# Attention stage of a hybrid layer: the order of VectorE, ScalarE and SyncE written out by hand

## The chip, the cores and the metric

The kernel runs on one core of a Trainium2 chip, as one program. The metric is the device time of one execution in microseconds. A core has TensorE (PE: matmuls and transpositions; PEld: its weight loads), VectorE (DVE), ScalarE (ACT), GpSimd (POOL) and SyncE (SP), which issues most of the transfers. Every engine takes its own instructions in the order in which the program lists them, and waits at each one for its inputs and for its output buffer.

## The reference, cut to what matters

```python
mod = c @ w_ada + b_ada; shift, scale, gate = split(mod, 3)
h = rmsnorm(x, norm_g) * (1 + scale) + shift            # 1024 tokens x 1024
glu_a, glu_b, z_conv, q, k, v, z_att, g_conv, g_att = split(h @ w_in)
u = conv31(glu_a * sigmoid(glu_b)) + conv_b
y_conv = (silu(layernorm(u)) * silu(z_conv)) @ w_conv_out
q, k = rope16(q), rope16(k)                             # 24 heads of 64, first 16 columns rotated
for g, (window, dilation) in enumerate(((128, 1), (512, 4), (2048, 16))):   # 8 heads each
    o[g], m[g], den[g] = banded_softmax_attention(q, k, v, window, dilation)  # max and sum kept
wt[g] = den[g] * exp(m[g] - max(m));  att = sum(wt[g] * o[g]) / sum(wt[g])
y_att = (att * silu(z_att)) @ w_att_out
merged = sigmoid(g_conv) * y_conv + sigmoid(g_att) * y_att
out = rmsnorm(x + gate * (merged @ w_o), final_g)
```

## The kernel before, in words

All matmuls are done to nearly full float32 precision: each operand is split into a high part (a ScalarE `Copy` into the 32-bit matmul type) and a low part (original minus high, on VectorE, or on GpSimd for most projection weights), and three matmuls (high x high, high x low, low x high) are summed in one PSUM bank. `split` at L55 writes both parts; L57 is the Copy and L58 the subtraction. `mm3` (L73 to L75) is the three matmuls.

The program runs in stages: the modulation and the normed input (to about 100 us), the projections of the convolution branch with the convolution on VectorE, the first output projection (to 639 us), the attention stage (639 to 1148 us), a merge (to about 1192 us) and the last projection with its norm. The change lies in the attention stage and, with one instruction, in the merge.

The attention stage (L645 to L1060) is cut into slots. A slot on TensorE is half of a half of a projection unit: 4 of 8 blocks of the contraction, 12 matmuls of 512 columns. There are 32 units of 4 slots: 24 make k and q (two for each of the 12 pairs of heads; the pairs run over four columns of heads j and in each over the three dilation groups g), and the last 8 make the gate of the attention branch. `pieces` (L769) yields after each slot, and, where a half of a unit is complete, hands back a function `after` that takes the result out of its bank (two banks, `pd2`). For part 0 of k and q that is the rotary part on VectorE (L720 to L723: shuffle, two multiplies, an add) and then the split (L731, L732); part 1 is split only. In the next slot SyncE copies the parts into the stacked tiles that the scores read (`move_kq`, L796: five transfers for each head, L794), the second head's later.

From slot 0 on, a slot also carries one of 8 steps of the current pair (r = 0 to 7 below): the scores (L862, L863), with the minimum and mask on VectorE (L866) and two Exp on ScalarE (L870); two slots later (`turn`) a transposition of the probabilities into a bank `t` (L878) and their split (tiles `ph`, `pl`); four slots later (`values`) the product with v (L896 to L898), whose bank ScalarE copies out every second slot (L902). The banks `s`, `t` and `o` have two buffers each. `load_v` (L811) loads half of a pair's v and splits it for its two heads. `store_stats` writes row minima and sums to memory, and after each group 2 `combine` (L910) brings the three groups of a column together: it loads the statistics, computes weights (L918 to L928), transposes them (L932) into a `t` bank, stores them, loads them back as rows (tiles `wg`, tag `wr`, two buffers) and weighs the outputs (L953 to L964); the last column goes straight into the tiles of the next projection, the others through memory. `load_raw` loads weights into a ring of three buffers.

The loop that lays this out (L1017 to L1058) stands in `tc.manual_schedule(engines={nc.tensor.engine})`: TensorE's order is as written, and the order of the other engines is chosen by a planner with costs of its own. The beginning of the program has all of TensorE, VectorE, ScalarE and SyncE in written order.

In the merge (L1074 to L1088) each of 8 blocks of the attention projection is multiplied by its gate, which comes from memory, and added to the other branch.

Of the kernel before, what the change touches and what calls it, by code (L numbers as in the profile page):

```python
# [39 lines left out]
def layer(ctx: ExitStack, tc: tile.TileContext, a, out):  # L40
# [621 lines left out]
    for x, dt, n in (("sb", F32, 3), ("ph", F32R, 2), ("pl", F32R, 2)):  # L662
        ap_.tile([P, 512], dt, name=x, tag=x, bufs=n)
# [42 lines left out]
    made, parts_of = [], {}  # L706

    class Parts:
# [7 lines left out]
        def __call__(self, half, s, ps):  # L716
            src = ps
            if self.part == 0:
                sh, src = (ap_.tile([P, 512], F32, name=x, tag="gs", bufs=2) for x in ("sh", "rot"))
                nc.vector.stream_shuffle(sh, ps, SHUF)  # L720
                nc.vector.tensor_mul(src, ps, ctab[:, s])
                nc.vector.tensor_mul(sh, sh, stab[:, s])
                nc.vector.tensor_add(src, src, sh)  # L723
            r = (1, 4, 16)[self.g]
            n = 512 // r

            def dst(t):
# [3 lines left out]
            nc.scalar.activation(dst(self.hi), src, AF.Copy)  # L731
            nc.vector.tensor_sub(dst(self.lo), src, dst(self.hi).bitcast(F32))  # L732
            if half:
                parts_of[self.n, self.part] = self.parts
                made.append((self.n, self.part))

    def gate(d):
# [18 lines left out]
    def units():  # L756

        raws = kq_raws(0)
        gates = list(range(KT))
        for n in range(12):  # L760
            yield kq_weights(raws, 0), Parts(n, 0)
            w = kq_weights(raws, 1)
            if n + 1 < 12:
                raws = kq_raws(n + 1)
            yield w, Parts(n, 1)
        for d in gates:
            yield weights(a["w_t"][60 + d], lo_eng=nc.gpsimd), gate(d)

    def pieces():  # L769

        source = units()
        ahead = next(source)
        while ahead:
            (hi, lo), consume = ahead
            ahead = next(source, None)
            for half in range(2):
                s = slice(half * 512, half * 512 + 512)
                ps = bank()
                for k in range(KT):
                    c = slice(k * P, (k + 1) * P)  # L780
                    mm3(ps, hi[:, c], lo[:, c], hh[:, k, s], hl[:, k, s], k == 0, k == KT - 1)
                    if k == 3:
                        yield
                yield lambda half=half, s=s, ps=ps: consume(half, s, ps)
# [21 lines left out]
    def row_tile(name):  # L806
        return ap_.tile([P, 512], F32, name=name, tag="wr", bufs=2)
# [3 lines left out]
    def load_v(n, half):  # L811
# [14 lines left out]
        for h in range(2):  # L826
            if not half:
                v2[n, h] = stk.tile([P, 8, 2, 64], F32R, name="vt", tag=f"v{turn_of(n, h)}")
            hi, lo = (v2[n, h][:, 4 * half:4 * half + 4, x] for x in range(2))
            split(hi, lo, raw[:, :, 64 * h:64 * h + 64])  # L830
            yield

    class Attend:
# [19 lines left out]
        def scores(self, st_):  # L853
# [4 lines left out]
            sb = self.sb[st_] = ap_.tile([P, 512], F32, name="sb", tag="sb", bufs=3)  # L858
# [45 lines left out]
        def store_stats(self):  # L904
            by_token(sscr[self.j][:, self.g], self.stats.rearrange("p t h x -> p t (h x)"), self.g)
            yield
# [3 lines left out]
    def combine(j):  # L910
# [24 lines left out]
        nc.sync.dma_start(wscr[j].rearrange("g h (t p) -> (g h t) p", p=P), wt)  # L935
        yield

        def row_of(g, s):
            row = row_tile("wg")
            for h in range(2):  # L940
                nc.sync.dma_start(row[64 * h:64 * h + 64], wscr[j][g, h:h + 1, s].to_broadcast([64, 512]))
            return row

        o = [o_of.pop((j, g)) for g in range(3)]
        halves = [slice(0, 512), slice(512, 1024)]
        rows = row_of(0, halves[0]), row_of(1, halves[0])
        yield
        for half, s in enumerate(halves):
            o0 = o[0][:, s]
            o1 = o[1].rearrange("p (r b i) -> p b i r", r=4, b=2)[:, half]  # L950
            o2 = o[2].rearrange("p (t s i) -> p i t s", t=8, s=2)[:, 32 * half:32 * half + 32]
            w0, w1 = rows
            nc.vector.tensor_mul(o0, o0, w0)  # L953
            w2 = row_of(2, s)
            v = w1.rearrange("p (i r) -> p i r", r=4)
            nc.vector.tensor_mul(v, v, o1)
            nc.vector.tensor_add(o0, o0, w1)
            gt = row_tile("gt")
            nc.sync.dma_start(gt, zascr[j][:, s])
            yield  # L960
            v = w2.rearrange("p (i t s) -> p i t s", t=8, s=2)
            nc.vector.tensor_mul(v, v, o2)
            nc.vector.tensor_add(o0, o0, w2)
            nc.vector.tensor_mul(o0, o0, gt)  # L964
            if not half:
                rows = row_of(0, halves[1]), row_of(1, halves[1])
            if j < 3:
                nc.sync.dma_start(atscr[j][:, s], o0)
            else:
                att_parts(3, s, o0)  # L970
            yield
# [3 lines left out]
    def att_parts(j, s, raw):  # L975
# [3 lines left out]
        split(ah[j][:, s], al[j][:, s], raw)  # L979
# [4 lines left out]
    def w_out(n, kp, pool=None):  # L984

        raw = load_raw(a["w_o"][n, kp])
        if pool:
# [6 lines left out]
        split(hi, lo, raw)  # L994
        woh[n, kp], wol[n, kp] = hi, lo

    stream = pieces()


# [3 lines left out]
    STEPS = (2, 3, 4, 5, 7, 8, 9, 10, 11)  # L1003
    beside, heads = {}, {}
# [9 lines left out]
    def v_slots(n, half):  # L1014
        return [8 * n + x for x in ((2, 4, 5) if half else (-2, 0, 1))]

    with tc.manual_schedule(engines={nc.tensor.engine}):  # L1017
        for slot_ in range(-LEAD, (2 * len(order) + KT) * 4 - LEAD):
            due, made[:] = made[:], []
            after = next(stream)  # L1020
            for n, part in due:
                move_kq(n, part, 0)
                in_steps(moves(n, part, 1), [slot_ if n == 0 else slot_ + 1 if part else 8 * n - 4])
            for half in range(2):
                n = (slot_ + 2) // 8
                if slot_ == v_slots(n, half)[0] and 0 <= n < len(order):
                    in_steps(load_v(n, half), v_slots(n, half))
            if 0 <= slot_ < stages:
                n, st_ = divmod(slot_, 8)
                if st_ == 0:  # L1030
                    heads[n] = Attend(n)
                heads[n].scores(st_)
                if st_ == 7:
                    in_steps(heads[n].store_stats(), [slot_ + 1])
                    if order[n][1] == 2:
                        in_steps(combine(order[n][0]), [slot_ + 1 + x for x in STEPS])
# [5 lines left out]
            if TURN <= slot_ < stages + TURN:  # L1042
                n, st_ = divmod(slot_ - TURN, 8)
                heads[n].turn(st_)
            for c in beside.pop(slot_, ()):
                next(c)
            j = slot_ - stages - VAL
            if 0 <= j < 3:
                raw = load_raw(atscr[j])
                for half in range(2):  # L1050
                    s = slice(half * 512, half * 512 + 512)
                    att_parts(j, s, raw[:, s])
            if j in (4, 6, 8):
                w_out(0, j // 2 - 2)
            if j == 11:
                ahead = weights(a["w_ao"][0], 512)
            if after:
                after()  # L1058
        assert not beside and next(stream, None) is None
    c_ctx.close()  # L1060
# [14 lines left out]
    for d in range(KT):  # L1075
# [3 lines left out]
        if d in (1, 3, 5):  # L1079
            w_out(*((0, 3), (1, 0), (1, 1))[d // 2], fp if d > 1 else None)  # L1080
# [10 lines left out]
    w_out(1, 2, fp)  # L1091
    w_out(1, 3)
# [115 lines left out]
```

## Time and profile before

| what | value |
|---|---|
| runs shown: median (lowest to highest) | 1286.9 us (1286.76 to 1290.35) |
| the profiled execution, its own time | 1287.98 us |
| its span, first to last instruction | 1286.2 us |
| TensorE busy | 1243.6 us, 97% |
| VectorE busy | 915.3 us, 71% |
| ScalarE busy | 516.6 us, 40% |
| GpSimd busy | 94.7 us, 7% |
| mean granted clock of TensorE | 0.992 |
| the chain that ended last, by engine | PE 81%, DVE 7%, ACT 5%, DMA 4%, issue 2% |

A busy share is the time in which an engine has an instruction under way. Matmuls overlap, so TensorE's own durations are longer than the distance from one start to the next; starts are what to measure by. The wait list says for each line how long its engine stood before it and which engine or transfer released it. The releaser is the one that came last by the profile; where that one had long been done, it was another. The granted clock is the share of full speed that TensorE was given in a stretch.

### The profile page before, as it was taken

Reading aid. Unit: us, or ns where it says so; the run is one execution under the profiler, and the core shown is the slowest. Engines: PE = TensorE matmul, PEld = TensorE weight load, DVE = VectorE, ACT = ScalarE, POOL = GpSimd, SP = SyncE. Lnnn points to the kernel's source line nnn. Section 1 sums busy time; section 2 is a strip of 40 time slices with the busy share of each in tenths; the row PEclk is TensorE's granted clock in tenths of the full one; section 3 lists DMA queues with packets and bytes.
Section 4 is the critical chain, followed back from the end, with each engine's and each line's share of the span. In section 5 each row is a group of like instructions: output and inputs, shape, how many; then the busy total and the mean of one; then the engine's idle time right before and its main releaser. Section 6 shows DMA issues by size and latency. Waiting matters only on the chain.

```text
span 1286.2 us, 16854 instructions
## 1 busy us (share of the span) xinstructions
PE 1243.6 (97%) x6208; PEld 1041.9 (81%) x6208; DVE 915.3 (71%) x1496; ACT 516.6 (40%) x1027; POOL 94.7 (7%) x79
## 2 busy tenths in 40 slices
PE   6999999999999999999999999999989999899997
PEld 4787888888888888888788888878878878788886
DVE  6777999999999987843255657857866753339544
ACT  4553112111222147620125656556556578324211
POOL 0000000000000000000230111111111102100000
PEclk9999999999999999999999999999999999999999
DMA  9522312211211122555655555475466464459231
GB/s 367 181 95 71 110 66 61 87 52 48 98 50 50 49 74 74 177 182 191 140 137 124 130 134 139 130 190 132 126 167 153 127 171 142 150 189 315 91 104 69
DMA packets 89751, 165.35 MB, mean 129 GB/s; under 512 B 28547, under 2 KB 42179, under 8 KB 89669
## 3 DMA queue, kind: packets, MB, share of 16 engines
q1 hardware_dynamic: 73248, 157.76, 40.9%
q10 hardware_dynamic: 16420, 6.51, 1.9%
q8 instruction: 49, 0.80, 0.3%
q14 instruction: 34, 0.27, 0.1%
HBM read 105.74 MB, written 27.04 MB: 103 GB/s over the span
## 4 chain that ended last, share of the span: by engine, by line
PE 81%; DVE 7%; ACT 5%; DMA 4%; issue 2%; ACTq 0%; SPq 0%; DVEq 0%
PE d L73 19%; PE d L74 19%; PE d L75 19%; PE d L1113 2%; PE d L1112 2%; PE d L467 2%; PE d L1111 2%; PE d L469 2%; PE d L468 2%; PE t L878 1%; ACT sb L870 1%; PE d L251 1%; PE s L863 1%; PE d L249 1%; PE d L250 1%
## 5 line engine op out<-in xcount | busy, mean ns | idle before, releaser
L73 PE MATMUL d<-hh,whi 128*128 128x512 f32 x1072 | 430.6, 402 | 4.8 <-ACT gs L740 3.9
L74 PE MATMUL d<-hl,whi 128*128 128x512 f32 x1072 | 420.4, 392 | 1.7 <-DVE hl L349 1.7
L75 PE MATMUL d<-hh,wlo 128*128 128x512 f32 x1072 | 420.8, 393 | 0.0
L408 DVE SCALAR_TENSOR_TENSOR v<-u,cw,v 128x1024 f32<-128x1024 f32 x232 | 280.5, 1278 | 0.0
L73 PEld LDWEIGHTS d<-hh,whi 128*128 128x128 f32 x1072 | 203.3, 190 | 45.3 <-ACT gs L740 4.7
L75 PEld LDWEIGHTS d<-hh,wlo 128*128 128x128 f32 x1072 | 202.8, 189 | 43.7
L74 PEld LDWEIGHTS d<-hl,whi 128*128 128x128 f32 x1072 | 203.7, 190 | 42.0 <-DVE hl L349 2.5
L57 ACT ACTIVATE whi<-wraw 128x512 fp32r<-128x512 f32 (+1 forms) x107 | 88.1, 834 | 238.1 <-PE d L74 219.0
L58 POOL TENSOR_TENSOR wlo<-wraw,whi 128x512 fp32r<-128x512 f32 (+1 forms) x56 | 85.7, 1542 | 669.7 <-ACT whi L57 629.1
L870 ACT ACTIVATE sb<-sb,stats 128x128 f32<-128x128 f32 (+1 forms) x192 | 85.0, 444 | 121.4 <-DVE stats L866 121.2
L58 DVE TENSOR_TENSOR pl<-t,ph 128x384 fp32r<-128x384 f32 (+2 forms) x96 | 52.3, 545 | 104.5 <-ACT ph L57 104.3
L58 DVE TENSOR_TENSOR wlo<-wraw,whi 128x1024 fp32r<-128x1024 f32 (+1 forms) x51 | 57.9, 1137 | 14.4 <-ACT whi L57 13.6
L866 DVE CUSTOM_DVE_ANT_0 sb<-s,mask 128x128 f32<-128x128 f32 (+1 forms) x192 | 59.3, 346 | 11.3 <-PE s L863 11.3
L862 PE MATMUL s<-k,q 128*128 128x128 f32 (+1 forms) x192 | 47.4, 270 | 7.6 <-DMA sscr<-stats 5.3
L897 PE MATMUL o<-ph,vt 128*64 128x128 f32 (+1 forms) x216 | 49.3, 239 | 3.5 <-DVE vt L58 3.5
L863 PE MATMUL s<-k,ql 128*128 128x128 f32 (+1 forms) x192 | 51.0, 279 | 0.2 <-DMA ql<-kqp 0.2
L1113 PE MATMUL d<-oh,hl 128*128 128x512 f32 (+1 forms) x136 | 51.2, 376 | 0.0
L1111 PE MATMUL d<-oh,hh 128*128 128x512 f32 (+1 forms) x136 | 51.2, 376 | 0.0
L896 PE MATMUL o<-ph,vt 128*64 128x128 f32 (+1 forms) x216 | 49.1, 238 | 2.1 <-ACT ph L57 1.4
L634 DVE TENSOR_TENSOR gs<-d,sgc 128x512 f32<-128x512 f32 x16 | 11.1, 691 | 54.9 <-PE d L75 54.9
L467 PE MATMUL d<-vh,hh 128*128 128x512 f32 x128 | 49.8, 389 | 0.0
L468 PE MATMUL d<-vl,hh 128*128 128x512 f32 x128 | 49.8, 389 | 0.0
(224 smaller groups left out, 1956.9 us busy)
## 6 DMA issues: line engine op xcount, KB each, us to landing
wraw<-in_w_t SPq DMA_DIRECT2D x67, 512.0 KB, 4.0
k<-kqp SPq DMA_DIRECT2D x96, 128.0 KB, 2.8
q<-kqp SPq DMA_DIRECT2D x96, 128.0 KB, 2.8
wa<-in_w_ada SPq DMA_DIRECT2D x16, 512.0 KB, 6.0
ql<-kqp SPq DMA_DIRECT2D x48, 128.0 KB, 2.6
wg<-wscr SPq DMA_DIRECT2D x48, 128.0 KB, 3.0
wraw<-in_w_v SPq DMA_DIRECT2D x11, 512.0 KB, 3.6
x<-in_xT SPq DMA_DIRECT2D x8, 512.0 KB, 10.2
```

The lines of the kernel that those rows point to most:

```text
L57: nc.scalar.activation(hi, raw, AF.Copy)
L58: (lo_eng or nc.vector).tensor_sub(lo, raw, hi.bitcast(F32))
L73: nc.tensor.matmul(ps, lh, rh, start=start, stop=False)
L74: nc.tensor.matmul(ps, lh, rl, start=False, stop=False)
L75: nc.tensor.matmul(ps, ll, rh, start=False, stop=stop)
L408: nc.vector.scalar_tensor_tensor(d, u[:, k:k + S], cw[:, ct, k:k + 1], d, op0=mult, op1=add)
L467: nc.tensor.matmul(ps, hh[:, k, ts_], rh, start=k == 0, stop=False)
L468: nc.tensor.matmul(ps, hh[:, k, ts_], rl, start=False, stop=False)
L863: nc.tensor.matmul(ps[:, c:c + w], ql[:, ts_], k[:, ks], start=False, stop=True)
L870: nc.scalar.activation(sb[:, c:c + w], sb[:, c:c + w], AF.Exp, bias=stats[:, t, h, 1:2], scale=-1.0, accum_out=stats[:, t, h, 0:1])
L1111: nc.tensor.matmul(ps, hh[:, k, c], rh, start=k == 0, stop=False)
L1113: nc.tensor.matmul(ps, hl[:, k, c], rh, start=False, stop=k == KT - 1)
```

## The change

What it does:

- VectorE, ScalarE and SyncE join TensorE in the written order of the attention stage.
- Low parts are written a slot late: `split_late` writes the high part at once and puts the subtraction on a list that opens the next slot. That holds for the probabilities, v, k and q, and the attention parts and some output weights at the end.
- Within a slot the order is now: late low parts, 12 matmuls, values, turn, scores, copies of k and q, `after`, the steps beside (v, combination, end weights), then weights prepared or loaded.
- The weights' raw transfers are issued two units' halves ahead (`raw_for(u + 2)`) and split one unit ahead (`prepare(u + 1)`); the loads of the end (`att_again`, `w_out`, `first_ao`) stand two slots ahead of their splits, at slots 101 to 111.
- The combination goes over 16 slots instead of 9 steps up to the 11th, weighs in the rows instead of in the outputs, with three row buffers; the score copy has two buffers instead of three. The store of its weights is issued by ScalarE.
- The gate is copied out without the Sigmoid; the Sigmoid is applied in the merge to the 128x1024 gate after its load.

```diff
+    def split_late(hi, lo, raw, then=None):
+        nc.scalar.activation(hi, raw, AF.Copy)
+        def low():
+            nc.vector.tensor_sub(lo, raw, hi.bitcast(F32))
+            if then:
+                then()
+        lows.append(low)
...
-            nc.scalar.activation(y, ps, AF.Sigmoid)
+            nc.scalar.activation(y, ps, AF.Copy)
...
+                yield (lambda half=half, s=s, ps=ps: consume(half, s, ps),
+                       lambda half=half, u=u: (raw_for if half else prepare)(u + 1 + half) if u + 1 + half < units else None)
...
-            split(hi, lo, raw[:, :, 64 * h:64 * h + 64])
+            split_late(hi, lo, raw[:, :, 64 * h:64 * h + 64])
...
-            split(hi[:, :o], lo[:, :o], ps[:, :o])
+            split_late(hi[:, :o], lo[:, :o], ps[:, :o])
...
-        nc.sync.dma_start(wscr[j].rearrange("g h (t p) -> (g h t) p", p=P), wt)
+        nc.scalar.dma_start(wscr[j].rearrange("g h (t p) -> (g h t) p", p=P), wt)
...
+        a0, a1, a2 = (row_of(g, 0) for g in range(3))
+        yield
+        weigh(a0, 0, 0)
+        weigh(a1, 1, 0)
+        nc.vector.tensor_add(a0, a0, a1)
+        yield
+        gt = gate_of(0)
+        weigh(a2, 2, 0)
+        nc.vector.tensor_add(a0, a0, a2)
+        yield
+        b0 = row_of(0, 1)
+        nc.vector.tensor_mul(a0, a0, gt)
+        yield
+        b1 = row_of(1, 1)
+        put(a0, 0)
+        yield
+        weigh(b0, 0, 1)
+        yield
+        b2 = row_of(2, 1)
+        weigh(b1, 1, 1)
+        nc.vector.tensor_add(b0, b0, b1)
+        yield
+        gt = gate_of(1)
...
-    STEPS = (2, 3, 4, 5, 7, 8, 9, 10, 11)
+    STEPS = (1, 2, 3, 4, 6, 7, 8, 9, 10, 11, 12, 13, 14, 15, 16)
...
+    for n in range(len(order)):
+        in_steps(load_v(n, 0), [8 * n + x for x in (-3, -1, 1)])
+        in_steps(load_v(n, 1), [8 * n + x for x in (1, 3, 5)])
+    for x, it in ((101, att_again(0)), (102, att_again(1)), (105, att_again(2)), (106, w_out(0, 0)), (109, w_out(0, 1)),
+                  (110, w_out(0, 2)), (111, first_ao())):
+        in_steps(it, [x, x + 2])
+    raw_for(0)
+    prepare(0)
+    with tc.manual_schedule(engines={nc.tensor.engine, nc.vector.engine, nc.scalar.engine, nc.sync.engine}):
+        for slot_ in range(-LEAD, 4 * units - LEAD):
+            due, lows[:] = lows[:], []
+            for low in due:
+                low()
+            after, prepared = next(stream)
             if VAL <= slot_ < stages + VAL:
                 n, st_ = divmod(slot_ - VAL, 8)
                 heads[n].values(st_)
...
             if TURN <= slot_ < stages + TURN:
                 n, st_ = divmod(slot_ - TURN, 8)
                 heads[n].turn(st_)
+            if 0 <= slot_ < stages:
...
+                heads[n].scores(st_)
+            for n, part in made:
+                move_kq(n, part, 0)
+                in_steps(moves(n, part, 1), [slot_ if n == 0 else slot_ + 1 if part else 8 * n - 4])
+            made[:] = []
+            if after:
+                after()
             for c in beside.pop(slot_, ()):
                 next(c)
+            if prepared:
+                prepared()
...
         nc.sync.dma_start(sg_, ascr[d])
+        nc.scalar.activation(sg_, sg_, AF.Sigmoid)
```

## Rows read from the trace of the kernel before

**Rows 1.** TensorE's timeline: start us, us, engine, line, operation; a clean and a stopped slot.

```profile
737.47 0.47 PE L73 MATMUL d<-hh,whi 128*128 128x512 f32 x1
...
740.32 0.22 PE L862 MATMUL s<-k,q 128*128 128x128 f32 x1
...
741.50 0.47 PE L73 MATMUL d<-hh,whi 128*128 128x512 f32 x1
...
836.65 0.48 PE L73 MATMUL d<-hh,whi 128*128 128x512 f32 x1
...
843.75 0.47 PE L73 MATMUL d<-hh,whi 128*128 128x512 f32 x1
```

**Rows 2.** TensorE's wait list, 636 to 1150 us: us in total, times, longest.

```profile
PE s L862 <- DMA sscr<-stats: 5.3, 2, 2.7
...
PE d L73 <- ACT gs L740: 3.9, 2, 3.4
...
PE o L897 <- DVE vt L58: 3.5, 3, 1.5
...
PE t L932 <- DVE pl L58: 3.0, 3, 1.1
...
PE s L862 <- DVE stats L866: 2.3, 1, 2.3
...
PE o L896 <- ACT ph L57: 1.4, 1, 1.4
...
PE o L896 <- ACT vt L57: 0.7, 1, 0.7
```

**Rows 3.** Windows after waits: busy us of each engine (instructions), granted clock, DMA.

```profile
677.00:685.00 8.00, 5.66 (x22) 4.54 (x21) 5.47 (x17) 6.52 (x16) 0.00 (x0) 0.79 0.38 83
...
1100.00:1112.00 12.00, 8.58 (x31) 6.52 (x30) 2.45 (x2) 4.88 (x7) 2.37 (x1) 0.86 0.46 147
```

**Rows 4.** Groups by line: shapes xcount | busy us, mean ns; ScalarE's table loads.

```profile
L740 ACT ACT_TABLE_LOAD x7 | 9.0, 1283 | 0.1
...
L870 ACT ACT_TABLE_LOAD x6 | 7.7, 1283 | 0.5 <-ACT gs L740 0.4
```

**Rows 5.** SyncE's queue: the last copy of q before a stopped slot.

```profile
941.24 0.51 SPq L794 DMA_DIRECT2D ql<-kqp  x1
```

**Rows 6.** Groups by line: reductions, low probabilities and weighings on VectorE.

```profile
L866 DVE CUSTOM_DVE_ANT_0 sb<-s,mask 128x128 f32<-128x128 f32 (+1 forms) x192 | 59.3, 346 | 11.3 <-PE s L863 11.3
...
L58 DVE TENSOR_TENSOR pl<-t,ph 128x384 fp32r<-128x384 f32 (+2 forms) x96 | 52.3, 545 | 104.5 <-ACT ph L57 104.3
...
L956 DVE TENSOR_TENSOR wg<-wg,oc 128x512 f32<-128x512 f32 x8 | 10.2, 1274 | 1.5 <-DMA wg<-wscr 1.5
...
L962 DVE TENSOR_TENSOR wg<-wg,oc 128x512 f32<-128x512 f32 x8 | 9.2, 1150 | 2.4 <-DMA wg<-wscr 2.4
```

**Rows 7.** Timelines of VectorE and ScalarE: one rotated half from shuffle to low part.

```profile
866.08 0.74 DVE L720 STREAM_SHUFFLE sh<-d 128x512 f32<-128x512 f32 x1
...
868.44 0.69 DVE L723 TENSOR_TENSOR rot<-rot,sh 128x512 f32<-128x512 f32 x1
...
869.17 1.12 ACT L731 ACTIVATE kqp<-rot 128x512 fp32r<-128x512 f32 x1 [0.39 <-DVE rot L723]
...
870.33 1.10 DVE L732 TENSOR_TENSOR kqp<-rot,kqp 128x512 fp32r<-128x512 f32 x1 [0.85 <-ACT kqp L731]
```

**Rows 8.** VectorE's timeline and a ScalarE group: the merge's first multiplies; a 128x1024 Copy.

```profile
1154.02 1.29 DVE L1084 TENSOR_TENSOR sgr<-d,sgr 128x512 f32<-128x512 f32 x2 [5.10 <-DMA sgr<-ascr]
...
L57 ACT ACTIVATE oh<-wraw 128x1024 fp32r<-128x1024 f32 x8 | 8.4, 1055 | 13.7 <-DMA wraw<-in_w_o 13.7
```

**Rows 9.** Timelines of GpSimd and VectorE: one addition beside GpSimd and one alone.

```profile
890.83 1.41 POOL L58 TENSOR_TENSOR wlo<-wraw,whi 128x512 fp32r<-128x512 f32 x1 [13.68 <-ACT whi L57]
...
891.00 1.26 DVE L925 TENSOR_TENSOR ma<-ma,sd 128x16 f32<-128x16 f32 x1
...
1093.18 0.17 DVE L925 TENSOR_TENSOR ma<-ma,sd 128x16 f32<-128x16 f32 x1
```

More of the change, by code (lines that the diff above doesn't have):

```diff
@@ L754, in kq_raws, with raw_for, prepare @@
         return [load_raw(a["w_t"][16 + 2 * n + i]) for i in range(2)]
[L756 to L767, printed above, removed]
-    def pieces():
[L771 to L775, printed above, removed]
+    raws, made_w = {}, {}
+    units = 2 * len(order) + KT
+    def raw_for(u):
+        if u >= 2 * len(order):
+            raws[u] = load_raw(a["w_t"][36 + u])
+        elif u % 2 == 0:
+            raws[u] = kq_raws(u // 2)
+    def prepare(u):
+        if u >= 2 * len(order):
+            hi = wpool.tile([P, 1024], F32R, name="whi", tag="whi")
+            lo = wpool.tile([P, 1024], F32R, name="wlo", tag="wlo")
+            split(hi, lo, raws.pop(u), nc.gpsimd)
+            made_w[u] = (hi, lo), gate(u - 2 * len(order))
+        else:
+            n, part = divmod(u, 2)
+            made_w[u] = kq_weights(raws[2 * n], part), Parts(n, part)
+    def pieces():
+        for u in range(units):
+            (hi, lo), consume = made_w.pop(u)
             for half in range(2):
@@ L806, in row_tile @@
     def row_tile(name):
[L807 removed]
+        return ap_.tile([P, 512], F32, name=name, tag="wr", bufs=3)
     shift_of = {}
@@ new lines, in put @@
+        def put(row, half):
+            s = slice(512 * half, 512 * half + 512)
+            if j < 3:
+                nc.sync.dma_start(atscr[j][:, s], row)
+            else:
+                att_parts(3, s, row)
+        a0, a1, a2 = (row_of(g, 0) for g in range(3))
+        yield
+        weigh(a0, 0, 0)
[6 more added lines that the diff above has]
+        yield
@@ new lines, in combine @@
+        b0 = row_of(0, 1)
[12 more added lines that the diff above has]
+        yield
+        weigh(b2, 2, 1)
+        nc.vector.tensor_add(b0, b0, b2)
+        yield
+        nc.vector.tensor_mul(b0, b0, gt)
+        yield
+        put(b0, 1)
+        yield
@@ L986, in w_out @@
         raw = load_raw(a["w_o"][n, kp])
+        if not pool and (n, kp) < (0, 3):
+            yield
         if pool:
@@ L1012, in moves @@
         yield
[L1014 to L1036, printed above, removed]
+    for n in range(len(order)):
[6 more added lines that the diff above has]
+    prepare(0)
+    stream = pieces()
+    with tc.manual_schedule(engines={nc.tensor.engine, nc.vector.engine, nc.scalar.engine, nc.sync.engine}):
[4 more added lines that the diff above has]
+            after, prepared = next(stream)
             if VAL <= slot_ < stages + VAL:
@@ L1044, in layer @@
                 heads[n].turn(st_)
+            if 0 <= slot_ < stages:
+                n, st_ = divmod(slot_, 8)
+                if st_ == 0:
+                    heads[n] = Attend(n)
+                heads[n].scores(st_)
[5 more added lines that the diff above has]
+                after()
             for c in beside.pop(slot_, ()):
                 next(c)
[L1047 to L1058, printed above, removed]
+            if prepared:
+                prepared()
+            if 0 <= slot_ < stages and st_ == 7:
+                heads[n].store_stats()
+                if order[n][1] == 2:
+                    in_steps(combine(order[n][0]), [slot_ + 1 + x for x in STEPS])
         assert not beside and next(stream, None) is None
+        for low in lows:
+            low()
+    ahead = ahead_ao[0]
     c_ctx.close()
```

92 lines of the change are left out of this document (47 added, 45 removed).

## The prediction

> **What bounds the kernel now.** I read the wait list of TensorE first, then the granted clock of the stretches around its waits, then the timelines of the other engines at those places. TensorE is the bound: in an undisturbed slot of the attention stage it runs without a hole, 12 projection matmuls in 740.32 - 737.47 = 2.85 us and the slot in 4.03 us [rows 1]. So a change can only win what TensorE loses in waiting, and the reader is to see in the wait list how little that is: 5.3 + 3.9 + 3.5 + 3.0 + 2.3 + 1.4 + 0.7 = 20.1 us in 13 waits [rows 2]. Two things come on top. The slot from 836.65 to 843.75 took 7.10 us, 3.07 more than the clean one, for a wait put at 2.57 [rows 1]; a wait costs about 1.2 times what the list says, 24.1 us in all. And after five of the longer waits the granted clock fell: in the first of these stretches it is 0.79 of full over 8 us, in the last 0.86 over 12 us, so some of each ran at 1.2 instead of 2.4 GHz [rows 3]. A stretch of T us at mean clock c loses (1 - c) x T there: 8 x 0.21 and 12 x 0.14 are both 1.7 us; five make 8.4. The bill is 24.1 + 8.4 = 32.5 us, and no rewriting of the order can win more.
>
> **The change part by part.** I split the bill by cause.
>
> *Scores before the rotation (bill 2.3 x 1.2 + 1.7 = 4.5).* In the first pairs VectorE ran the rotary part of a projection ahead of the reduction that frees a score bank. In the written order the reduction of a slot stands ahead of that slot's rotation. One 1.28 us table load [rows 4] for the first Exp stays on ScalarE; I leave 0.5 as a rest. Bounds of the rest: 0 to 4.5.
>
> *Transfers (5.3 x 1.2 + 1.7 = 8.1).* The two waits that the profile puts on a statistics store are waits for copied k and q: the last copy of low q was issued at 941.24 [rows 5], and TensorE stood in that slot. SyncE had been holding the copies behind stores and loads of the combination. Written out, each set of five copies is issued in the slot after its low part, three or more slots (12 us) before the scores that read it. What stands ahead of them now, in program order: the v load (waits for the low part of the v half before, one slot), the combination's row loads (wait for a freed row), the weight loads (wait for GpSimd). Each of these frees within one to two slots, so I take the whole 8.1. If a wait on SyncE holds four slots, it all comes back.
>
> *Low parts a slot late (3.5 + 0.7 for v, x 1.2 + 1.7 = 6.7; probabilities 1.4 x 1.2 + 1.7 = 3.4).* The low part of v is now the first work of the next VectorE slot, two to four slots before the values matmul reads it: 6.7 goes. The late probabilities came from ScalarE, which switched tables between Exp and the gates' Sigmoid: 7 + 6 loads of 1.28 us [rows 4], 16.7 us. With a Copy in the gates these go, and 3.4 with them; the three slots there have 12 us of TensorE work to hide one Copy each.
>
> *The last gates (3.9 x 1.2 + 1.7 = 6.4).* A gate's bank was freed late because ScalarE stood behind a weight that was still in transfer. Now the load is issued two slots (5.7 us and more) ahead and the bank's Copy stands before the split. But SyncE's queue is tighter: the weights of the last two units are loaded into a buffer that is free only when GpSimd has made the low part before, and stand behind row loads. I leave a rest of 1.0, bounds 0 to 6.4 and, if both units are late, 2 x (3 + 1.7) = 9.4.
>
> *The combination over 16 slots (3.0 x 1.2 = 3.6 stays; new waits).* The transposition of the combination's weights takes a bank that is free when the low probabilities of the slot before are made. Their subtraction now comes after the combination's weight step on VectorE, so the wait of about 1 us, three times, stays: rest 3.6. The price of the new order lies in the pair of heads after it. Count from the end of TensorE's slot 5, slots of 4.03 us, with these durations: two reductions 2 x 0.35 = 0.7 and low probabilities 0.55 [rows 6]; rotation 869.13 - 866.08 less 0.4 of reductions = 2.6, its high part on ScalarE 1.12, low part 1.10 [rows 7]; weighings 1.27 and 1.15 [rows 6], contiguous multiply or add 0.7 to 1.15 (two in 1.29 [rows 8]), v's low part 0.4 (estimated by width from the 0.55). Slot 6 (TensorE ends 4.0): reductions to 4.7, rotation to 7.3, ScalarE's high part to 8.45. Slot 7 (8.1): low probabilities to 7.85, then the queue stands until 8.45 for the high part, low part to 9.55, reductions 10.25, weighing of two groups and their sum to 13.1. Slot 8 (12.1): low probabilities 13.65, v 14.05, reductions 14.75, rotation 17.35, third group 19.4. Slot 9: low probabilities of slot 8 at 20.0. TensorE reads them in slot 10, at 16.1 + 2.85 = 18.95: a new wait of 1.05. Behind it in VectorE's queue stand the kq low part and the reductions, but their readers come a slot or more later, so one wait is the price. Lower bound 0 (slots of group 0 run longer than 4.03); upper bound with two collisions with GpSimd, 2 x 1.09 more (below), and the clock lost: 1.05 + 2.2 + 1.7 = 5.0. I take 1.5, near the walk: 3 x 1.5 = 4.5. In the pairs without combination the same walk has no 2.85 and 2.05 us of weighing, starts slot 8's reductions at 12.1 and ends at 15.95, 3 us before TensorE asks. The fourth combination runs beside the gates, and nothing of attention waits for it.
>
> *Sigmoid in the merge (0).* Eight Sigmoids of 128x1024, each about the 1.06 us of the same shape [rows 8], and one table load, 9.8 us of ScalarE beside 192 matmuls of 2.85/12 us, 46 us. Cover: VectorE starts the merge 5.10 us late on the gate's transfer already [rows 8], and eight banks hold four output blocks of TensorE's work. Start about 2.4 later, no hole. Without the cover 2.4; a gain has no source.
>
> *Edits at nothing.* TensorE's matmuls are the same in number, only values, transpositions and scores change places within a slot. The score copy in two buffers instead of three holds, since its transposition now stands before the scores that reuse it. The combination's store of weights goes from SyncE to ScalarE: four issues of about 0.5 us (the nearest row, a copy's issue [rows 5]), hidden under TensorE's slot of 4.03 us each time; without that cover 4 x 0.5.
>
> Sum: rests 0.5 + 0 + 0 + 1.0 + 3.6 + 4.5 = 9.6, so 32.5 - 9.6 = 22.9 us. The profiled execution took 1287.98 us (span 1286.2): 1265.1 by that, and as the median 1286.9 lies 1.1 lower, 1264.
>
> **A rule against it.** VectorE's three-operand steps are not of one length: the same 128x16 addition took 0.17 us in one place and 1.26 where GpSimd had started its subtraction 0.17 us earlier [rows 9]. The Trainium skill (SBUF — State Buffer, section SBUF: two separate sides) says that VectorE with two SBUF inputs and GpSimd lock each other out of a shared port pair for a whole instruction. The trace agrees. By rows alone: the written order puts GpSimd's two weight splits into slots 2 and 6, right beside rotation, kq low part and weighing. If both hit in every combination, its term is 3 x 5.0 instead of 4.5: 10.5 us more. This is a rival below.
>
> **The rivals.** (A) *GpSimd collides in each combination*: 1264 + 10.5 = 1274.5. For it: the two additions of [rows 9]; against it: such collisions lie in the waits of before as well. (B) *SyncE's waits move rather than go*: one transfer waits in order and the copies or weights behind it come late. Then the 8.1 stays and the last gates cost 2 to 9 more: 1264 + 8.1 + 4 = 1276. For it: all of SyncE is now bound to one order; against it: distances of 3 slots and more. (C) *Slower: VectorE's lag carries over.* If the chain reduction, rotation, ScalarE's high part, low part does not fit two slots plus the 2.85 us of slack (10.9 us), TensorE waits at each of the 24 rotated halves. The chain measured is 0.7 + 2.6 + 1.12 + 1.10 and again 0.7, with low probabilities and v 1.0: 7.2 us. It decides from 3.7 us more, that is three to four collisions each time. Price 24 x 1.5 = 36 us with the clock lost, over the bill of 32.5: about 1290. (D) *The change does nothing*, because the planner had found nearly this order and other waits take the place: 1286.
>
> **How the numbers follow.** Forecast 0.60; A 0.13; B 0.15; C 0.06; D 0.06. Own range of the forecast: no rest but the transposition, 1258, to 4 more than summed, 1271. The 8-in-10 range goes from the bill with hardly a rest (32.5 - 2, 1256) over A and B to 1279. A change under 0.3% (3.9 us) can't be told from none here. Faster 0.90 (forecast, A, B and little of D), same 0.05, slower 0.05.
>
> **What would show it.** In TensorE's wait list of the changed kernel: no wait for v, for k and q copies, for the score bank, or for gate banks; the three waits at the transposition still there; three new ones for low probabilities, put on VectorE, two to three slots after a change of pair. ScalarE's table loads in the attention stage down from 13 to one or two. The granted clock at 1.00 in nearly all stretches between 670 and 1120 us. The merge without a hole on TensorE although VectorE starts later. Wrong would be waits for transfers anywhere in the stage, or a wait in every pair of heads.

## The result, and the profile after

| | median of the runs | lowest to highest | runs |
|---|---|---|---|
| before | 1287.31 us | 1285.45 to 1290.35 | 8 |
| after | 1280.9 us | 1276.08 to 1282.71 | 8 |

The ratio is 0.9942, with a 95% interval of 0.9925 to 0.9959: faster by 6.4 us, where 22.9 were forecast, and outside the range. The profiled execution after took 1280.72 us (span 1278.9). From its first projection matmul to the first of the merge the attention stage fell from 508.5 to 501.2 us; what follows it took 138.7 before and 139.6 after.

TensorE's wait list after, 636 to 1150 us (us in total, times, longest), is the whole of it:

```profile
PE t L947 <- DVE pl L713: 10.9, 3, 3.7
PE o L914 <- DVE pl L713: 2.3, 3, 0.8
PE d L75 <- POOL wlo L58: 1.9, 2, 1.1
PE d L73 <- DVE gs L634: 0.9, 1, 0.9
```

All causes of [rows 2] but one are gone: no wait for k, q or v, for a score bank, for high probabilities or a gate's bank (L634 belongs to the branch before). L947 is the transposition of the combination's weights, L932 before: 3.0 us there, 10.9 now. TensorE's timeline after shows one of the three, in slot 28 of the stage, then one of the three new waits for low probabilities:

```profile
781.89 0.40 PE L73 MATMUL d<-hh,whi 128*128 128x512 f32 x1
...
785.97 0.28 PE L879 MATMUL s<-k,ql 128*128 128x256 f32 x1
789.89 0.27 PE L947 MATMUL t<-ident,w 128*48 128x128 f32 x1 [3.64 <-DVE pl L713]
789.92 0.47 PE L73 MATMUL d<-hh,whi 128*128 128x512 f32 x1
...
817.15 0.33 PE L914 MATMUL o<-pl,vt 128*64 128x256 f32 x1 [0.78 <-DVE pl L713]
```

The last score matmul of the slot starts at 785.97 and the transposition at 789.89. From start to start the slot takes 8.03 us; the least that the same slot of the four columns of heads takes is 4.20. The stretches behind the three stops, and the one between the first two, by windows (columns as in [rows 3]):

```profile
785.00:800.00 15.00, 11.36 (x69) 9.57 (x68) 8.96 (x25) 8.06 (x24) 3.01 (x2) 0.89 0.31 70
800.00:889.00 89.00, 88.22 (x551) 75.66 (x549) 64.38 (x172) 52.38 (x148) 15.08 (x10) 1.00 0.62 163
889.00:905.00 16.00, 12.33 (x67) 10.18 (x64) 9.33 (x26) 8.44 (x23) 2.98 (x2) 0.79 0.29 64
...
995.00:1011.00 16.00, 12.46 (x74) 10.59 (x73) 9.64 (x31) 8.75 (x26) 2.78 (x2) 0.89 0.34 80
```

The clock is at full between the stops and below it only behind them. Stops and clock together, slot by slot: 3.83 + 1.64, 4.00 + 2.83 and 3.72 + 1.52 = 17.5 us.

Why the weights are late is read from the queues that lead to them. The statistics load leaves SyncE behind five copies of k and q and a v load:

```profile
776.15 1.66 SPq L810 DMA_DIRECT2D k<-kqp  x2
...
779.11 0.59 SPq L810 DMA_DIRECT2D ql<-kqp  x1
779.81 0.54 SPq L680 DMA_DIRECT2D vr<-vscr  x1
780.39 0.56 SPq L928 DMA_DIRECT2D sd<-sscr  x1
```

VectorE's timeline, from the low part of v that frees the v load's buffer to the weights, and further down the queue ahead of the late low probabilities:

```profile
779.06 0.43 DVE L713 TENSOR_TENSOR vt<-vr,vt 128x256 fp32r<-128x256 f32 x1 [0.79 <-ACT vt L710]
...
783.62 0.18 DVE L933 TENSOR_TENSOR ma<-sd 128x16 f32<-128x16 f32 x1 [3.44 <-DMA sd<-sscr]
...
786.33 0.69 DVE L841 TENSOR_TENSOR vr<-vr,row 128x512 f32<-128x512 f32 x1
786.93 1.27 DVE L938 TENSOR_TENSOR sd<-sd 128x48 f32<-128x48 f32 x1
...
788.94 0.24 DVE L943 TENSOR_TENSOR w<-sd,ma 128x48 f32<-128x48 f32 x1
789.06 0.68 DVE L713 TENSOR_TENSOR pl<-t,ph 128x512 fp32r<-128x512 f32 x1
...
814.68 1.09 DVE L974 TENSOR_TENSOR wg<-wg,oc 128x512 f32<-128x512 f32 x1
...
816.41 0.68 DVE L713 TENSOR_TENSOR pl<-t,ph 128x512 fp32r<-128x512 f32 x1
...
1147.74 1.29 DVE L1149 TENSOR_TENSOR sgr<-d,sgr 128x512 f32<-128x512 f32 x2 [1.68 <-ACT sgr L1134]
```

v's low part ends near 779.5, the copies are issued by 779.7, the v load goes out at 779.81 and the statistics load at 780.39; VectorE goes on with it at 783.6. Until then VectorE stands at L933 for 3.44 us, and a slot's reductions, low parts and v work queue up behind it. ScalarE stands too: the Exp of the weights waits 2.29 us for VectorE, with the high parts of the next projection weights behind it.

```profile
784.28 0.25 ACT L936 ACTIVATE sd<-sd 128x48 f32<-128x48 f32 x1 [2.29 <-DVE sd L935]
```

VectorE's queue runs from 784 on, the weights' step after the rest. Right behind the weights, at 789.06, come the low probabilities that free the transposition's bank; they end at 789.74, and TensorE, which has stood since 786.25, transposes at 789.89. VectorE's own wait list has this standing three times; in the profile before, that load cost VectorE 2.1 us, once, at the fourth column:

```profile
DVE ma L933 <- DMA sd<-sscr: 10.4, 3, 3.6
```

ScalarE's groups after: one table load is left of the 13 [rows 4], and the Sigmoid stands in the merge.

```profile
L1134 ACT ACTIVATE sgr<-sgr 128x1024 f32<-128x1024 f32 x8 | 8.5, 1057 | 6.0 <-DMA sgr<-ascr 6.0
...
L886 ACT ACT_TABLE_LOAD x1 | 1.3, 1283 | 0.0
L1134 ACT ACT_TABLE_LOAD x1 | 1.3, 1283 | 0.0
```

### The profile page after: what moved, and what is told of

Same layout as the page of the kernel before. It is cut to its first block, busy times and chain, and to the rows that moved or that the text cites. A ratio compares the mean times of both kernels' runs of the same rounds, so it can differ in the third digit from the quotient of the medians.

```text
span 1278.9 us, 16967 instructions
## 1 busy us (share of the span) xinstructions
PE 1241.3 (97%) x6208; PEld 1035.5 (81%) x6208; DVE 916.1 (72%) x1496; ACT 510.4 (40%) x1023; POOL 98.1 (8%) x79
## 4 chain that ended last, share of the span: by engine, by line
PE 87%; DVE 6%; DMA 3%; ACT 1%; issue 1%; SPq 0%; POOL 0%; DVEq 0%; ACTq 0%; POOLq 0%
PE d L73 21%; PE d L75 21%; PE d L74 21%; PE d L1178 2%; PE d L1177 2%; PE d L468 2%; PE d L467 2%; PE d L1179 2%; PE d L469 2%; PE t L894 2%; PE s L879 1%; PE s L878 1%; PE o L914 1%; PE o L912 1%; PE o L913 1%
## 5 line engine op out<-in xcount | busy, mean ns | idle before, releaser
L73 PE MATMUL d<-hh,whi 128*128 128x512 f32 x1072 | 423.4, 395 | 0.9 <-DVE gs L634 0.9
L58 POOL TENSOR_TENSOR wlo<-wraw,whi 128x512 fp32r<-128x512 f32 (+1 forms) x56 | 89.0, 1607 | 660.5 <-ACT whi L57 615.9
L58 DVE TENSOR_TENSOR wlo<-wraw,whi 128x1024 fp32r<-128x1024 f32 (+1 forms) x50 | 57.2, 1145 | 14.5 <-ACT whi L57 13.9
L710 ACT ACTIVATE ph<-t 128x384 fp32r<-128x384 f32 (+2 forms) x96 | 45.6, 475 | 53.1 <-PE t L894 45.2
L878 PE MATMUL s<-k,q 128*128 128x128 f32 (+1 forms) x192 | 54.8, 310 | 0.0
L634 DVE TENSOR_TENSOR gs<-d,sgc 128x512 f32<-128x512 f32 x16 | 11.1, 691 | 54.9 <-PE d L75 47.1
L74 PE MATMUL d<-ul,whi 128*128 128x512 f32 x128 | 49.8, 389 | 0.0
```

What stands on the lines that cost most here:

```text
L58: (lo_eng or nc.vector).tensor_sub(lo, raw, hi.bitcast(F32))
L73: nc.tensor.matmul(ps, lh, rh, start=start, stop=False)
L74: nc.tensor.matmul(ps, lh, rl, start=False, stop=False)
L878: nc.tensor.matmul(ps[:, c:c + w], q[:, ts_], k[:, ks], start=True, stop=False)
```

## The experiments

The theory after this reading: VectorE stands in written order for the statistics load, and that alone is most of the missing gain. First come two ways to take it away, and the Sigmoid by itself. Each kernel was timed beside the one before (medians of 1286.0 to 1287.1 us in the three groups of runs; the last three kernels ran on another chip), and the ratios are to that.

**The load a slot earlier** (`e1_stats_early`)

```diff
-    STEPS = (1, 2, 3, 4, 6, 7, 8, 9, 10, 11, 12, 13, 14, 15, 16)
+    STEPS = (0, 2, 3, 4, 6, 7, 8, 9, 10, 11, 12, 13, 14, 15, 16)
```

> The changed kernel with the statistics of a finished column loaded one slot earlier (first step in slot 0 of the next pair instead of slot 1); nothing else moves. Theory S (VectorE stands 3.3 to 3.6 us for this load, and the low probabilities that free the transposition's bank stand behind it): VectorE's wait for the load goes, the three waits of TensorE at the transposition of the combination's weights fall from 10.9 us to about 1 each, 3 in all, the clock stays up after them, and the time falls by 8 + 6 = 14 us to about 1267. Rival Q (it is the place of the low part behind the weight step in VectorE's queue, load or no load): the waits stay above 2 each and the time at 1277 or more.

1273.22 us, ratio 0.9894 (0.9873 to 0.9915). TensorE's list and VectorE's, each from this kernel:

```profile
PE t L947 <- DVE pl L713: 6.3, 3, 2.4
```

```profile
DVE ma L933 <- DMA sd<-sscr: 0.7, 1, 0.7
```

VectorE's standing went from 10.4 to 0.7 us and TensorE's only from 10.9 to 6.3: half of the 14 us of theory S, and more than the 4 that rival Q left. VectorE's and SyncE's timelines have the rest:

```profile
785.85 0.69 DVE L841 TENSOR_TENSOR vr<-vr,row 128x512 f32<-128x512 f32 x1 [1.80 <-DMA vr<-vscr]
786.46 0.20 DVE L938 TENSOR_TENSOR sd<-sd 128x48 f32<-128x48 f32 x1
```

```profile
775.12 0.38 SPq L928 DMA_DIRECT2D sd<-sscr  x1
775.59 1.00 SPq L62 DMA_DIRECT2D wraw<-in_w_t  x2
...
780.02 0.55 SPq L680 DMA_DIRECT2D vr<-vscr  x1
```

Now the first step of v (L841), ahead of the weights in VectorE's queue, stands 1.80 us for its own load. The early statistics load itself is the likely reason: it waits on SyncE until 775.12 for the statistics to be stored (9.4 us), and the two weight loads behind it, both out by 769.5 in the kernel after, go out at 775.59 and 776.21. The v load is then issued at 780.02 with these weights still under way and takes 5.8 us until VectorE goes on, against 3.5 in the kernel after. L938 takes 0.20 us here, where it took 1.27 beside GpSimd's subtraction in the kernel after.

**The transposition a slot later, and both** (`e2_turn_late`, `e3_both`)

```diff
-    STEPS = (1, 2, 3, 4, 6, 7, 8, 9, 10, 11, 12, 13, 14, 15, 16)
+    STEPS = (1, 2, 3, 5, 6, 7, 8, 9, 10, 11, 12, 13, 14, 15, 16)   # e2_turn_late
+    STEPS = (0, 2, 3, 5, 6, 7, 8, 9, 10, 11, 12, 13, 14, 15, 16)   # e3_both
```

> The changed kernel with the transposition of the combination's weights (and its copy and store) one slot later, slot 5 instead of slot 4. Theories S and Q agree here: the low probabilities and the weights are ready a slot (4.2 us) before TensorE asks, the three waits go, VectorE still stands 3.4 us each time for the statistics. 10.9 us of waiting and about 6 of clock go: about 1264. Rival M (the wait only moves): with VectorE late by the same 3.4 us, the next low probabilities are late for the values matmul and most of the 17 us comes back there: 1275 or more.

> Both: statistics loaded a slot earlier and the transposition a slot later. By S the two remove the same loss, so this is not faster than the better of the two by more than 3 us (the 1 us that is left at each transposition): 1263 to 1265. If each removes a loss of its own, it is 8 us or more below both.

1268.48 us, ratio 0.9858 (0.9839 to 0.9877), and 1263.4 us, ratio 0.9821 (0.9803 to 0.984). With the transposition a slot later VectorE stands for the load as long as ever (10.5 us, four times) and TensorE does not wait at L947 at all. Rival M did not happen: the waits for low probabilities stay at 2.4 us. But five waits for GpSimd's weights, 6.1 us, come instead, and the time is 4.5 us above the expected 1264: ScalarE still stands 6.7 us, three times, for L935 with the weights' high parts behind it, and GpSimd follows those. With both, TensorE's list is:

```profile
PE o L914 <- DVE pl L713: 2.4, 3, 0.8
PE d L75 <- POOL wlo L58: 1.9, 2, 1.1
PE d L73 <- DVE gs L634: 0.9, 1, 0.9
```

With both, ScalarE does not stand for L935 any more, and GpSimd's waits are back at 1.9 us. So the two are 5.1 us below the better one, more than the 3 that theory S allowed, and far from the 8 of two losses of their own. The stage takes 484.5 us, 16.7 less than in the kernel after, against 17.5 counted for the three stops. So the stops are the missing gain.

**The weights ahead of v** (`e6_weights_first`, on top of the early load)

```diff
-            for c in beside.pop(slot_, ()):
+            steps = list(beside.pop(slot_, ()))
+            for c in steps[::-1] if slot_ % 8 == 3 else steps:
```

> The kernel with early statistics, and in slot 3 of a pair the combination's weights made ahead of the v half's steps instead of behind them. Theory D (what is left of the wait at the transposition, 6.3 us in 3, is again a transfer in VectorE's queue: 1.80 us for the v half that was loaded late): VectorE makes the weights in that time, the wait falls from 2.1 to about 1 each, and the time from 1273.2 to about 1268, the clock staying up. Rival Q (the low part that frees the bank stands last in any case, and it is what TensorE waits for): 2 us each as before and 1272 to 1274, since the v half's addition still stands ahead of the low part.

1268.18 us, ratio 0.9873 (0.9843 to 0.9903). TensorE's list:

```profile
PE t L947 <- DVE pl L713: 3.1, 3, 1.1
```

With neither load in VectorE's way the stops shrink to the 1 us each that the prediction had kept; each slot is 1.2 us too long and the clock holds.

**The two halves of the change alone** (`e4_sigmoid_only`: before, with the Sigmoid moved; `e5_order_only`: after, with it back)

```diff
-            nc.scalar.activation(y, ps, AF.Sigmoid)
+            nc.scalar.activation(y, ps, AF.Copy)
...
         nc.sync.dma_start(sg_, ascr[d])
+        nc.scalar.activation(sg_, sg_, AF.Sigmoid)
```

(the same two places, reversed, for `e5_order_only`)

> The kernel before with one part of the change alone: the gates copied out without the Sigmoid, the Sigmoid in the merge. The prediction's account gives this part 3.4 us (late probabilities) and, of the 6.4 of the last gates, perhaps half, since ScalarE stood there for a weight in transfer and not for a table: 1281 to 1284 against 1287.3. Rival (the table loads were hidden but for the one wait, and the Sigmoid in the merge makes VectorE later): 1287 and no gain.

> The changed kernel with the Sigmoid back in the gates: the written order alone. If the two parts of the change add, the 8.2 us that the Sigmoid's move gave alone (1286.0 to 1277.8) are missing here, and the written order by itself is slower than before: 1287 to 1290, with waits for gate banks or late probabilities in TensorE's list. Rival: the written order hides the table loads by itself (the Copy that frees a bank stands early, and loads are two slots ahead): 1281 to 1283, the Sigmoid's move being worth nothing in it.

1277.76 us, ratio 0.9931 (0.9912 to 0.995), and 1282.85 us, ratio 0.9973 (0.9958 to 0.9987). The Sigmoid alone took the wait for late probabilities and half of that for the gates, from 3.9 to 1.8 us in TensorE's list:

```profile
PE d L73 <- ACT gs L740: 1.8, 2, 1.0
```

It is worth 8.2 us on the kernel before, more than expected: part of that is a fall of the clock that the profile of before has behind the first scores and this profile has not (the last section). Under the written order, which removes the same gate waits by itself, it is worth 2 us by the medians and 4 by the ratios. Alone, the written order is 3.5 us faster than before and not slower. The parts do not add.

**The Sigmoid back in the better order** (`e11_sigmoid_back`: `e3_both` with `Sigmoid` in the gates, none in the merge)

> The kernel with both moves, with the Sigmoid back in the gates (13 or so more table loads in the stage, none in the merge). Against 1263.4. Alone on the kernel before, the move of the Sigmoid was worth 8.2; in the changed kernel it was worth about 2, beside waits of 3.6 us for the weights. Theory: those waits hid it; with them gone the late probabilities come back and the move is worth 4 to 8 again: 1267 to 1271. Rival: the written order itself, with ScalarE's work of a slot fixed ahead of the gates, covers the table loads, and the move is worth 0 to 2: 1263 to 1265.5.

1267.85 us, ratio 0.9855 (0.9836 to 0.9873): 4.4 more than `e3_both`. The size is the theory's, its place is not: no probabilities are late, GpSimd's weights are.

```profile
PE d L75 <- POOL wlo L58: 4.1, 5, 1.1
```

ScalarE's timeline has the cause: a table load ahead of the gate, and the weight's high part behind both.

```profile
1047.39 1.28 ACT L750 ACT_TABLE_LOAD   x1
1048.68 0.60 ACT L750 ACTIVATE gs<-d 128x512 f32<-128x512 f32 x1
1049.75 1.06 ACT L57 ACTIVATE whi<-wraw 128x1024 fp32r<-128x1024 f32 x1 [0.47 <-ACT gs L750]
```

The remaining runs go after the waits that `e3_both` still has.

**Turn before values, and the combination spread** (`e7_turn_first`, `e8_spread`, each on `e3_both`)

```diff
+            if TURN <= slot_ < stages + TURN:          # e7: these three lines stand
+                n, st_ = divmod(slot_ - TURN, 8)       # ahead of the values
+                heads[n].turn(st_)
...
-    STEPS = (0, 2, 3, 5, 6, 7, 8, 9, 10, 11, 12, 13, 14, 15, 16)
+    STEPS = (0, 2, 3, 5, 6, 7, 9, 10, 11, 12, 13, 14, 15, 16, 17)   # e8, and prepared as in e9
```

> The fastest so far (early statistics, late transposition of the weights, 1263.4) with the transpositions of a slot ahead of its values matmuls instead of between values and scores. Theory T: the slots of group 2 are 0.06 us longer than in the kernel before (3.81 against 3.75) because the first score matmul behind a transposition starts late (0.31 us mean against 0.27); with values behind the transpositions the same step falls there instead: no gain, 1263 to 1264. Rival: it comes from the score operands and goes with the order: 32 slots x 0.06 = 2 us, 1261.5.

> The fastest so far with its two remaining kinds of wait taken away: the third group's weighing goes from slot 0, where VectorE also rotates, to slot 1, and all later steps of the combination with it (last step 17); and before slot 0 the next unit's weights are split ahead of the result that a slot evacuates. The three waits for low probabilities (2.4 us) and the two for GpSimd's low part of a weight (1.9 us) go, 4.3 us and a little for the dispatch: 1258 to 1259. Rival (the wait moves to the next slot, where the low part of k and q and the weighing meet): 1262 to 1264.

1268.11 us, ratio 0.9859 (0.9836 to 0.9883), and 1267.05 us, ratio 0.9851 (0.9827 to 0.9876): both slower than `e3_both`, which no expectation had. With turn first the last four slots of the third group take 3.86 us, against 3.80 in `e3_both` and 3.74 before. Spreading moved the waits two slots on and made them longer:

```profile
PE o L914 <- DVE pl L713: 4.5, 3, 2.1
```

Both waits for GpSimd's weights are gone in it. Its profile, the fastest of its four runs (1264.67 us, mean clock 0.999), has the stage as long as in `e3_both` (483.8 us) and loses 1.8 behind it, where a matmul of the merge waits 1.54 us; the other three runs have mean clocks of 0.995 to 0.997. How much of the rest is clock is not shown.

**Weights prepared earlier, and one weighing later** (`e9_weights_ahead` on `e3_both`; `e10_weigh_later` on that)

```diff
+            if prepared and slot_ < 0:                 # e9
+                prepared()
             for n, part in made:
...
-            if prepared:
+            if prepared and slot_ >= 0:
...
         gt = gate_of(0)
+        yield                                          # e10
         weigh(a2, 2, 0)
         nc.vector.tensor_add(a0, a0, a2)
-        yield
         b0 = row_of(0, 1)
```

> The kernel with both moves (1263.4), and in the slots before slot 0 the weights of the next unit are prepared ahead of the copies and the rotation, as in the spread-out kernel, where the two waits for GpSimd's low parts were gone. Theory: these two waits (1.9 us of idle, +1.0 us in slot -7 and +1.4 us in slot 1) go alone, and the three waits for low probabilities stay at 0.8 each: 1261, L75's waits under 0.3 us in all. Rival: the lag moves, ScalarE's splits of weights delay the first rotations and scores, a new wait of 1 to 3 us stands between slot -4 and slot 4, and the time stays at 1263 to 1265.

> The same, and in the combination the weighing of the third group with its addition moves from step 8 to step 9 (the gate's load stays in step 8). Theory, by the walk of the prediction: VectorE then makes the low probabilities of slot 8 at about 17.9 us instead of 20, ahead of TensorE's 18.95, so the three waits of L914 for low probabilities (2.4 us of idle, 3.0 with what follows) go: 1258. Rival: VectorE only carries the 2 us into the next slot and the low probabilities of slot 9 are late instead, three waits of 0.5 to 2 us a slot on, 1261 or more.

1261.25 us, ratio 0.9804 (0.9788 to 0.9821): both waits for GpSimd are gone and the stage is 2.5 us shorter, as the theory had it. 1260.03 us, ratio 0.9794 (0.9779 to 0.981): the stage is 1.7 us shorter again, half of what was expected. TensorE's list of the last kernel:

```profile
PE o L914 <- DVE pl L713: 1.1, 4, 0.4
```

Three of these waits stand one slot further on and cost 0.45 us each. The rival was right about the place, the theory about half of the gain. This kernel is the fastest run here: 27 us below the one before, 21 below the one after.

## Why the prediction was wrong

**The step that failed** is "*The combination over 16 slots*", in its first sentences: "the wait of about 1 us, three times, stays: rest 3.6". It measured 17.5 us. The working let VectorE arrive with a slot's normal load, and its slot-by-slot walk began at slot 6, where the weighing starts. In slots 1 to 4 of the same pair the written order binds the statistics load to VectorE's queue, and neither the load's 3.2 us from issue to landing nor its place on SyncE, behind the copies and the v load, was asked for. The instruction that frees the bank was named rightly, the low probabilities behind the weight step; what was missed is that this whole queue would be late. In the profile before nothing warned of it in the list that the prediction read, because VectorE took that load's result when it was there. The runs show its pieces: the load a slot earlier gives 7.7 us (1280.9 to 1273.2); on top of that the weights ahead of v give 5.0 (to 1268.2), or, in their place, the transposition a slot later 9.8 (to 1263.4).

The other terms, slots measured against the same slots of the four columns:

| term | predicted rest | measured |
|---|---|---|
| bill of before | 32.5 | 32.9 |
| first scores | 0.5 | 0 |
| k and q transfers | 0 | 0 |
| v; probabilities | 0; 0 | 0; 0 |
| last gates | 1.0 | 0 |
| transposition | 3.6 | **17.5** |
| low probabilities after it | 4.5 | 3.0 |
| GpSimd's weights at the start | not a term | 2.5 |
| slots without a stop | not a term | 2.3 longer |
| what follows the stage (Sigmoid in merge) | 0 | 0.9 |

In the stage alone 22.9 us were forecast and 508.5 - 501.2 = 7.3 came, 15.6 less; the terms give 13.9 + 2.5 + 2.3 - 1.5 - 1.0 - 0.5 - 0.4 = 15.3. What lies outside the stage cancels in the two profiles: 0.9 us more behind it and 1.0 less ahead of it, where nothing was changed. The medians are 6.4 apart and the profiled runs 7.3.

**What was right.** The bill and its causes held, but for the last gates: the working put their wait down to a weight in transfer, and half of it went with the Sigmoid alone. With the stops taken out the kernel takes the forecast time, 1263.4 against 1264. That agreement has luck in it: no rest at the transposition (3.6 less than forecast) and less for the low probabilities, but the two terms that were missing. The walk named the place of the waits for low probabilities, and its 1.05 us came out as 1.0 in each of three slots, but by luck: two errors cancel. TensorE's slots 30 to 33 take 4.20 to 4.39 us instead of 4.03, so it asks 1.4 us later than walked. VectorE is 1.1 us later than walked, because its first two weighings ran beside GpSimd in all three combinations:

```profile
805.45 3.58 POOL L58 TENSOR_TENSOR wlo<-wraw,whi 128x512 fp32r<-128x512 f32 x2 [17.32 <-ACT whi L57]
...
806.75 3.23 DVE L974 TENSOR_TENSOR wg<-wg,oc 128x512 f32<-128x512 f32 x2
```

The second of them took 2.17 us of the 3.23, and takes 1.10 in the second half of the combination with GpSimd idle. Without the collision there would have been no wait at all (an estimate from these durations; no run shows it). The eight Sigmoids in the merge cost nothing that shows: VectorE's first multiply waits 1.68 us and TensorE 0.3 us, once, in all of merge and last projection; `e4_sigmoid_only` has the Sigmoid in the merge too, and after the stage it takes 138.6 us, as before. I count the 0.9 us as the scatter of single profiles.

**The rivals.** B saw the kind of fault, "one transfer waits in order" and the others behind it come late, but priced the transfers of k, q and the gates, which are all in time. What came late, behind those copies, was a load whose reader is VectorE. A happened in each combination, beside the weighing as it was named, with the longer slots covering most of it. It also hit the weights' step: L938 beside GpSimd's subtraction took 1.27 instead of 0.20 us in the chain to the weights. It agrees with the port rule of the Trainium skill (SBUF — State Buffer, section SBUF: two separate sides) and is 1.1 us of each 3.6 us stop. C did not happen: no wait in every pair of heads. As what would be wrong the prediction named waits for transfers on TensorE; here the transfer stopped VectorE, and TensorE's list names VectorE's low probabilities: these do free the bank last, but they were late only because they had stood in the queue behind the load's reader.

**What stays open.** The third group's slots are some 0.06 us longer than before. The group of the first score matmul, now issued right behind a transposition, has a mean of 310 ns, in the profile after:

```profile
L878 PE MATMUL s<-k,q 128*128 128x128 f32 (+1 forms) x192 | 54.8, 310 | 0.0
```

and of 270 in the profile before:

```profile
L862 PE MATMUL s<-k,q 128*128 128x128 f32 (+1 forms) x192 | 47.4, 270 | 7.6 <-DMA sscr<-stats 5.3 <-DVE stats L866 2.3
```

Turn ahead of values did not give it back, but it moved the step: by starts, in the last four slots of the third group, the scores behind a transposition take 0.48 us (0.39 before, behind the projection), and in `e7_turn_first` the values behind it take 0.44 instead of 0.36, with the scores at 0.45. So what follows a transposition takes 0.08 us more in both orders; why, and why the scores stay long behind the values, is open. The old order of the three, under the new order of the other engines, was not tried.

## What to carry to other kernels

When engines go from a planned to a written order, walk every slot for every engine, and at each instruction that reads a transfer ask when the transfer was issued, behind what, and when it lands: an in-order engine stands there with all that is queued behind. An instruction off the critical path with a short list entry before (2.1 us, once) can become the bound; give its load a slot more, or its reader on the critical engine a slot more. Do not carry the price of a part from one kernel to another: the Sigmoid's move was worth 8.2, 4.4 or 2 to 4 us, depending on what else had removed the same waits. When a load is moved up, ask what it now holds back in its own queue: the early statistics load sent the weights out late, and the v load then landed late behind them.

## What the runs showed of the hardware

The clock fell behind stops of TensorE that differ little. In `e1_stats_early` it stood 1.90, 2.02 and 2.39 us at the three transpositions; these are the 12 us behind each:

```profile
788.00:800.00 12.00, 11.65 (x71) 10.02 (x72) 7.20 (x23) 6.13 (x18) 0.00 (x0) 1.00 0.44 113
...
889.00:901.00 12.00, 11.63 (x64) 9.89 (x65) 5.64 (x20) 5.62 (x17) 0.00 (x0) 0.86 0.38 89
...
992.00:1004.00 12.00, 11.68 (x64) 9.96 (x65) 5.65 (x20) 5.67 (x17) 0.00 (x0) 0.86 0.38 89
```

Behind the first all 12 us ran at 2.4 GHz, behind the other two part of them at 1.2 GHz, 12 x 0.14 = 1.7 us lost each. Behind the 1.0 us stops of `e6_weights_first` nothing was lost. The length of a stop does not decide it. Before the first scores TensorE stood 2.34 us in the kernel before and in `e4_sigmoid_only`; these are the two stops in the timelines, and the windows behind them, first of the kernel before, then of `e4_sigmoid_only`:

```profile
680.66 0.53 PE L862 MATMUL s<-k,q 128*128 128x256 f32 x1 [2.34 <-DVE stats L866]
...
680.05 0.39 PE L862 MATMUL s<-k,q 128*128 128x256 f32 x1 [2.34 <-DVE stats L866]
```

```profile
680.00:695.00 15.00, 14.34 (x79) 12.61 (x80) 8.16 (x29) 9.53 (x29) 2.59 (x2) 0.89 0.62 141
...
680.00:695.00 15.00, 14.95 (x90) 13.07 (x91) 7.93 (x26) 10.92 (x33) 2.59 (x2) 1.00 0.71 179
```

Behind the same stop one kernel lost 1.7 us to the clock and the other nothing. In the kernel before the clock also held behind a stop of 2.57 us (at 842) and fell behind one of 1.43 (at 1076); in `e8_spread` it held behind 2.11. What does decide no run here shows, so 1.7 us for each longer wait is a price that may come or not. The measure that the prediction took from before (1.2 times the list and 1.7 us for a fall) gives 10.9 x 1.2 + 3 x 1.7 = 18.2 us for the three stops of the kernel after, near the 17.5 measured: on the sum of three the price of a wait was right, and its length was not foreseen.
